# Input rows added onto folded row blocks in SBUF, gate products one per item, and four steps later in their queues

## The chip, the core and the metric

The kernel runs on one core of a Trainium2 chip. The metric is the device time of one launch in microseconds (us), the median of three runs: 2029.12 us before the change (2028.1 to 2029.63). All arithmetic is in 32-bit floats; TensorE products are made with three products of split operands (a high part and a low part), so a product in the text is often three matrix instructions.

## The reference

One layer of an encoder is computed for two sequences of 1024 rows by 1024 columns (`x_prompt`, `x_sample`):

```python
h = rmsnorm(x, g_mix) * (1.0 + sc1) + sh1
z = h @ w_in                          # q_lat 256, kv_lat 128, k_pe 64, f_in 512
y_mla = mla_group(q_lat, kv_lat, k_pe, ...)   # 4 heads, 1024 x 1024 softmax each
y_four = fourier_group(f_in, w_four)          # 2-D Fourier transform, real part
x = x + ga1 * (concatenate([y_mla, y_four]) @ w_out)
h2 = rmsnorm(x, g_ffn) * (1.0 + sc2) + sh2
ffn = (silu(h2 @ w_gate) * (h2 @ w_up)) @ w_down
out = rmsnorm(x + ga2 * ffn, g_final)
```

The shifts, scales and gates (`sh1`, `sc1`, `ga1`, ...) come from a conditioning vector of each sequence.

## The kernel before

There are five stages. Stage 1 normalises x and projects it. Stage 2 (to about 304 us) makes the Fourier part, already multiplied by its rows of `w_out` and by the gate, and stores it to DRAM as `fo_d`, 1024 x 1024 for each sequence. Stage 3 (about 304 to 720 us) is attention. Stages 4 and 5 are the feed-forward part, whose large products are made by a Strassen scheme of seven block products; it begins at about 745 us.

Stage 3 walks over 64 items: sequence s (2), block b of 256 query rows (4), head h (4), half u (2). The loop is at L1305. For item k it makes the scores (L1187 to L1221: score products in PSUM, maximum, exponential on ScalarE, reciprocal and normalisation on VectorE at L1215), turns the probabilities of an earlier item with TensorE transposes (`flip_p`, L1223), and after each pair of heads multiplies them by the values (`values`, L1237). For the heads listed in `COPIED` (L36), the probabilities first go through a copy by DMA on SyncE's queue (`pr<-p`, L1218), so that the transposes read them in another type. Meanwhile, items 3 and 4 of a block make the rotary part of the next block's queries (`rope_q`, L835, whose sum at L849 is on GpSimd), and odd items the absorbed queries (`absorb_q`, L864, tile `qa`).

The output projection of a block runs one to two blocks later (`out_step`, L1165, where i counts items from the start of the block, less one item where the block's second pair of heads is copied). It loads 128 rows of the Fourier part (`out_load`, L1118, into one of two buffers named `x2`), adds the projected attention onto it (`out_proj`, L1124, the sum at L1131 on VectorE), stores it and computes its root mean square (`norm2`, L1133: square on ScalarE, small operations of `rstd` on GpSimd), scales it (L1144; the step is kept in `S["scale"]` and taken out in the next item, L1316), and turns it for the feed-forward part (`flip_h`, L1151).

The input x has to be added to these rows. Before the change that is done in DRAM: `add_x` (L799) issues sixteen DMAs on GpSimd's queue, each adding 256 x 512 values of x onto `fo_d`. A one-element operation on the reciprocal of the item (`place`, L805) keeps each at its place in the queue, listed by item at L1300.

The gated output weights are made in stage 3 as well, once for each sequence: `gate_half` (L1251) loads half of a gate row for all partitions, `wv_load` (L1273) loads four tiles of weights and multiplies each by it on GpSimd (L1279), and `wv_split` (L1282) splits the products into high and low parts on ScalarE and VectorE. The combinations for the Strassen scheme of the first sequence are made by `comb_h` (L1255) on GpSimd, in two steps an item apart.

At the end of stage 3 the last block of the second sequence is treated apart: `x3_load` (L1405) loads its rows, `norm3` (L1424) normalises them, and `flip2` (L1442) turns the rows of the block before it, between the four output projections of the last block (loop at L1484). Its result goes through a tile `H40` that is written again soon after.

What sets the order: every engine and every DMA queue works in order. The order in a queue is made when the kernel is built, by a planner that takes what is ready first in its own estimate and goes by program order only among what is ready; so a DMA without anything to wait for can stand far ahead of its place in the program. `tc.issue_after(ins)` ties the instructions of its block behind `ins`, but only those that are on the same engine as `ins`. `here[...]` keeps the last instruction of a kind: `here["nb"]` and `here["v"]` are on VectorE, `here["exp"]` and `here["a"]` on ScalarE, `here["p"]` on GpSimd, `here["pe"]` on TensorE.

Of the kernel before, what the change touches and what calls it, by code (L numbers as in the profile page):

```python
# [12 lines left out]
F32 = mybir.dt.float32  # L13
# [3 lines left out]
ALU = mybir.AluOpType  # L17
# [4 lines left out]
P = 128  # L22
# [31 lines left out]
def hybrid_encoder_kernel(ctx: ExitStack, tc: tile.TileContext, a: dict):  # L54
# [741 lines left out]

    S = {}

    def add_x(i):  # L799

        s, b, g = i // 8, i // 2 % 4, i % 2
        bs = slice(256 * b, 256 * b + 256)
        gs = slice(512 * g, 512 * g + 512)
        pc = tiny.tile([P, 1], F32, name="pc")
        place = nc.gpsimd.tensor_tensor(out=pc, in0=S["rr"], in1=S["rr"], op=ALU.add).ins  # L805
        with tc.issue_after(place):
            nc.gpsimd.dma_start(fo_d[s][bs, gs], xs[s][bs, gs], accum_op=ALU.add)

    def half(name):
        return e.tile([P, 512], F32, tag="hv", name=name, bufs=2)  # L810
# [307 lines left out]
    def out_load(s, b, u):  # L1118
        r0 = (2 * b + u) * P
        x2 = tl.tile([P, D], F32, tag="x2", name="x2", bufs=2)  # L1120
        nc.sync.dma_start(x2, fo_d[s][r0 : r0 + P, :])
        S["x2", s, b, u] = x2
# [40 lines left out]
            nc.sync.dma_start(h2_d[s][:, 4 * g : 4 * g + 4, r0 : r0 + P], ht)  # L1163

    def out_step(s, b, i):  # L1165
        if i in (9, 11):
            out_load(s, b, i // 2 - 4)
        if i in (10, 12, 15, 16):
            n = (10, 12, 15, 16).index(i)
            out_proj(s, b, n // 2, n % 2)  # L1170
        if i in (12, 16):
            norm2(s, b, i // 4 - 3, tl, True)
        if i in (14, 19):
            flip_h(s, b, int(i == 19))

    with ExitStack() as st:
# [96 lines left out]
        def wv_load(s, g):  # L1273
            gs = slice(512 * g, 512 * g + 512)
            raw4 = (w if s == 0 else e).tile([P, 4, 512], F32, tag=f"lat{1 - s}{g}", name="wvr4")
            for h in range(HEADS):
                raw = raw4[:, h, :]
                nc.sync.dma_start(raw, wo_d[:, h, gs])
                nc.gpsimd.tensor_tensor(out=raw, in0=raw, in1=S["ga"], op=ALU.mult)  # L1279
                S["wv", h, g] = raw  # L1280

        def wv_split(i):  # L1282
            h, g = i % 4, i // 4
# [2 lines left out]
                split(wv[0][:, h, gs], wv[1][:, h, gs], S.pop(("wv", h, g)))  # L1286

        todo = {k: [] for k in range(nit)}
        for g in range(2):
            todo[2 * g].append(lambda g=g: gate_half(0, g))  # L1290
            todo[2 * g].append(lambda g=g: wv_load(0, g))
            todo[34 + 3 * g].append(lambda g=g: gate_half(1, g))
            todo[34 + 3 * g].append(lambda g=g: wv_load(1, g))
        for i in range(8):
            todo[40 + i // 2].append(lambda i=i: wv_split(i))
            todo[3 + i].append(lambda i=i: wv_split(i))
        for c, k in enumerate((49, 51, 57, 59)):
            todo[k].append(lambda c=c: comb_h(0, c))
            todo[k + 1].append(lambda: S.pop("comb")())
        for i, k in enumerate((6, 8, 10, 12, 17, 18, 19, 25, 26, 27, 33, 34, 35, 41, 42, 43)):  # L1300
            todo[k].append(lambda i=i: add_x(i))
        for u in range(2):
            todo[60 + u].append(lambda u=u: out_load(1, 2, u))

        for k in range(nit + 4):  # L1305
            if k >= nit:
                i = k - nit
                out_proj(1, 2, i // 2, i % 2)
                S["tail", i] = here["v"]
                if i == 1:  # L1310
                    norm2(1, 2, 0, tl)
                    S["tail", 5], S["tail", 6] = here["n"]
            if k < nit:
                s, b, h, u = items[k]
                scores(s, b, h, u)
                if "scale" in S:  # L1316
                    with tc.issue_after(here["nb"]):
                        S.pop("scale")()
                if k == nit - 1:
                    with tc.issue_after(here["exp"]):  # L1320
                        nc.scalar.activation(tiny.tile([P, 1], F32, tag="pc", name="warm"), cmask[:, 0:1], AF.Silu)
                nxt = items[k + 8 - k % 8] if k + 8 - k % 8 < nit else None
                i = k % 8
                if nxt is not None:
                    if i == 0:
                        load_q(*nxt[:2])
                    if i == 3 and nxt[1] == 0:
                        load_seq(nxt[0], [w.tile([P, 2, N], F32R, tag=f"lat1{i}", name=f"lat1{i}") for i in range(2)])
                    if i in (3, 4):
                        rope_q(*nxt[:2], i - 3, gbank)  # L1330
                    if i in (5, 6):
                        rope_flip(*nxt[:2], i - 5, tbank("pqt", F32R))
                if u == 1 and k + 1 < nit:
                    absorb_q(*items[k + 1][:3], gbank)
            for q in sorted({(k - 6) // 4, (k - 5) // 4}):
                if q >= 0 and k == (nit + 2 if q == nit // 4 - 1 else 4 * q + 5 + (q in COPIED)):
                    values(*divmod(q // 2, 4), q % 2)
                if k == nit + 2:
                    S["tail", 4], S["tail", 7] = here["v"], here["a"]
            for j in (k - 2, k - 1):  # L1340
                if 0 <= j < nit and j == k - 1 - (j // 4 in COPIED):
                    flip_p(*items[j])
                if k == nit:
                    S["tail"] = here["a"], here["v"]
            for n in (k // 8 - 1, k // 8 - 2):
                if 0 <= n < NOUT:
                    out_step(*divmod(n, 4), k - 8 * n - (2 * n + 1 in COPIED))
            for f in todo.get(k, ()):
                f()

    with ExitStack() as st:
# [53 lines left out]
        def x3_load():  # L1405
            X1 = quad("X1").rearrange("p a b -> p (a b)")
            for u in range(2):
                xn = X1[:, D * u : D * u + D]
                x2 = tl.tile([P, D], F32, tag="o0", name="x3", bufs=3) if u == 0 else xn
                nc.sync.dma_start(x2, fo_d[1][(6 + u) * P : (7 + u) * P, :])  # L1410
                S["x2", 1, 3, u] = x2
                S["xn", 1, 3, u] = xn

# [70 lines left out]
        for n in range(4):  # L1484
            out_proj(1, 3, n // 2, n % 2)
            if n == 1:
                norm3(0)
            if n == 2:
                fw = [tl.tile([P, 2, 512], F32R, tag=f"o{i}", name=f"fw{i}", bufs=3 - i) for i in range(2)]
                for i in range(2):  # L1490
                    split(fw[0][:, i, :], fw[1][:, i, :], w0[i])
            prep_step((2, 0, 1, 0)[n])
            if n == 1:
                hts = quad("H40")
                chained(flip2, 2, [S.pop(("xn", 1, 2, u)) for u in range(2)], lambda: tbank("pht").rearrange("p a b -> p (a b)"),
                        lambda g: hts[:, g, :])
                hts = None
# [493 lines left out]
```

## Time and profile before

| | before |
|---|---|
| median of three runs | 2029.12 us (2028.1 to 2029.63) |
| profiled execution | 2030.94 us |
| its span, first to last instruction | 2029.2 us |
| TensorE busy | 1981.6 us |
| VectorE, ScalarE, GpSimd busy | 1414.1, 896.7, 833.5 us |
| HBM read, written | 256.46 MB, 120.39 MB |
| mean granted TensorE clock | 0.994 |

In the rows, PE is TensorE, PEld its weight loads, DVE VectorE, ACT ScalarE, POOL GpSimd, SP SyncE; a q behind a name is the queue in which that engine issues DMAs. L1131 is line 1131 of the kernel. A timeline row has the start and the duration in us, the engine, the line, the operation, what it writes and reads, how many were merged, and in brackets the idle time of the engine before it with what ended that. A stretch row has the stretch, its length, the busy time and number of instructions of PE, PEld, DVE, ACT and POOL, the granted share of the TensorE clock, the share of the DMA engines' time and GB/s. A waiting row has the total, the number and the longest wait. A queue row has the number of packets, MB, and the share of the sixteen DMA engines' time. An issue row has the size and the median time from issue to landing.

### The profile page before, as it was taken

To read this page: it belongs to the slowest core of one execution; us is meant where nothing else is said; L and a number is where in the kernel's file an instruction comes from. 1 tells how busy PE (TensorE), PEld (TensorE's weight loads), DVE (VectorE), ACT (ScalarE), POOL (GpSimd) and SP (SyncE) were. 2 spreads that over 40 slices of the span, in tenths; PEclk is the share of its full clock that TensorE was granted. 3 is DMA by queue.
4 is the path that set the end of the run, shared out by engine and by line. 5 is a ranking of instruction groups with operands and counts; after the bars stand their busy time and mean duration, and the time that the engine had idled before them with its cause. 6 is when DMAs were issued, how large, how long until landed. Compare 5 with 4: busy or idle time off the path is not lost.

```text
span 2029.2 us, 28475 instructions
## 1 busy us (share of the span) xinstructions
PE 1981.6 (98%) x9840; PEld 1617.7 (80%) x9840; DVE 1414.1 (70%) x2088; ACT 896.7 (44%) x1733; POOL 833.5 (41%) x1013
## 2 busy tenths in 40 slices
PE   8899999999999999999999999999999999999997
PEld 7688877788887777888888888877788888888876
DVE  5677758676676779888677587677756655657684
ACT  4565545455465564333333364453333333336451
POOL 2454123112313327879878411233654454410142
PEclk9999999999999999999999999999999999999999
DMA  9685793667674575555555597664422322358762
GB/s 376 208 290 170 255 346 105 195 187 206 170 209 136 183 279 193 198 167 195 198 174 195 166 311 249 221 224 148 141 93 103 115 93 103 113 182 274 227 225 89
DMA packets 187725, 391.32 MB, mean 193 GB/s; under 512 B 19196, under 2 KB 58876, under 8 KB 183484
## 3 DMA queue, kind: packets, MB, share of 16 engines
q1 hardware_dynamic: 168908, 331.69, 48.4%
q0 software_dynamic: 18672, 57.81, 9.7%
q8 instruction: 77, 1.26, 0.3%
q14 instruction: 68, 0.56, 0.1%
HBM read 256.46 MB, written 120.39 MB: 186 GB/s over the span
## 4 chain that ended last, share of the span: by engine, by line
PE 55%; DVE 2%; DMA 2%; POOL 1%; issue 1%; ACT 0%; SPq 0%; DVEq 0%; ACTq 0%; POOLq 0%
PE bank L85 18%; PE bank L84 18%; PE bank L86 18%; DVE wl L64 1%; DMA draw<-t_d 1%; DVE val L144 1%; POOL val L144 1%; DMA val<-x_d 0%; DVE val L1788 0%; ACT wh L63 0%; POOL rs_y L111 0%; DMA draw<-s_d 0%; DVE val L1762 0%; SPq L1747 0%; DVE val L1777 0%
## 5 line engine op out<-in xcount | busy, mean ns | idle before, releaser
L84 PE MATMUL bank<-H,wh 128*128 128x512 f32 x1224 | 477.3, 390 | 5.3 <-DVE val L144 5.3
L86 PE MATMUL bank<-H,wl 128*128 128x512 f32 x1224 | 476.3, 389 | 0.2 <-DVE wl L64 0.2
L85 PE MATMUL bank<-H,wh 128*128 128x512 f32 x1224 | 476.3, 389 | 0.0
L144 DVE TENSOR_TENSOR val<-bank,val 128x512 f32<-128x512 f32 x244 | 166.8, 688 | 172.0 <-PE bank L86 169.1
L84 PEld LDWEIGHTS bank<-H,wh 128*128 128x128 f32 x1224 | 229.7, 188 | 56.3 <-DVE val L144 6.9
L86 PEld LDWEIGHTS bank<-H,wl 128*128 128x128 f32 x1224 | 229.8, 188 | 48.9 <-DVE wl L64 1.0
L85 PEld LDWEIGHTS bank<-H,wh 128*128 128x128 f32 x1224 | 229.8, 188 | 47.3
L64 DVE TENSOR_TENSOR wl<-draw,wh 128x512 fp32r<-128x512 f32 x286 | 202.3, 740 | 86.1 <-ACT wh L63 85.4
L63 ACT CAST wh<-draw 128x512 fp32r<-128x512 f32 x286 | 169.0, 620 | 159.9 <-PE bank L85 86.3
L85 PE MATMUL bank<-wl,wh 128*128 128x512 f32 x572 | 223.8, 391 | 3.6 <-DVE wl L64 3.6
L144 POOL TENSOR_TENSOR val<-val 128x512 f32<-128x512 f32 x58 | 84.3, 1461 | 339.9 <-DVE val L1762 189.2
L86 PE MATMUL bank<-wh,wl 128*128 128x512 f32 x572 | 222.7, 389 | 0.0
L84 PE MATMUL bank<-wh 128*128 128x512 f32 x572 | 222.6, 389 | 0.0
L63 ACT CAST wh<-rgu 128x512 fp32r<-128x512 f32 x171 | 106.3, 623 | 248.7 <-PE bank L85 192.3
L64 DVE TENSOR_TENSOR wl<-val,wh 128x512 fp32r<-128x512 f32 x133 | 134.9, 1016 | 70.8 <-ACT wh L63 70.5
L64 DVE TENSOR_TENSOR wl<-rgu,wh 128x512 fp32r<-128x512 f32 x171 | 165.3, 967 | 5.3 <-ACT wh L63 5.3
L63 ACT CAST wh<-val 128x512 fp32r<-128x512 f32 x133 | 82.3, 622 | 178.9 <-PE bank L85 158.6
L141 POOL TENSOR_TENSOR val<-rgu 128x512 f32<-128x512 f32 x80 | 114.4, 1430 | 97.1 <-DMA rgu<-in_wgu_dram 83.8
L85 PEld LDWEIGHTS bank<-wl,wh 128*128 128x128 f32 x572 | 107.4, 188 | 29.6 <-DVE wl L64 7.4
L84 PEld LDWEIGHTS bank<-wh 128*128 128x128 f32 x572 | 107.4, 188 | 22.5
L86 PEld LDWEIGHTS bank<-wh,wl 128*128 128x128 f32 x572 | 107.4, 188 | 21.8
L141 POOL TENSOR_TENSOR val<-val 128x512 f32<-128x512 f32 x89 | 119.2, 1357 | 1.3
(395 smaller groups left out, 3915.2 us busy)
## 6 DMA issues: line engine op xcount, KB each, us to landing
rgu<-in_wgu_dram SPq DMA_DIRECT2D x86, 512.0 KB
draw<-s_d SPq DMA_DIRECT2D x143, 256.0 KB
s_d<-val POOLq DMA_DIRECT2D x88, 256.0 KB, 3.6
draw<-t_d SPq DMA_DIRECT2D x88, 256.0 KB
pr<-p SPq DMA_DIRECT2D x40, 512.0 KB
s_d<-val SPq DMA_DIRECT2D x66, 256.0 KB
wada<-in_wa_dram SPq DMA_DIRECT2D x16, 1024.0 KB
draw<-in_w_down_dram SPq DMA_DIRECT2D x55, 256.0 KB
```

The costliest lines, as they stand in the source:

```text
L63: here["a"] = nc.scalar.copy(hi, src).ins
L64: here["v"] = nc.vector.tensor_tensor(out=lo, in0=src, in1=rd(hi), op=ALU.subtract).ins
L84: nc.tensor.matmul(out, lh, rh, start=first, stop=False, skip_group_check=cont)
L85: nc.tensor.matmul(out, lh, rl, start=False, stop=False, skip_group_check=cont)
L86: here["pe"] = nc.tensor.matmul(out, ll, rh, start=False, stop=last, skip_group_check=cont).ins
L141: return eng.tensor_tensor(out=out, in0=x, in1=y, op=ALU.subtract).ins
L144: return eng.tensor_tensor(out=out, in0=x, in1=y, op=ALU.add).ins
```

## The change

The sum with x moves from DRAM to SBUF: after `out_load` has loaded 128 rows of the Fourier part into `x2`, `add_x` lets a DMA on GpSimd's queue add the 128 x 1024 values of x onto that tile. There are again sixteen such DMAs of 512 KB, and the one-element operations that placed the old ones are gone. `out_load` of a block's first half moves one item earlier. The rows of the last two blocks are treated in the same way.

The products with the gate leave `wv_load` and become steps of their own (`wv_gate`), listed one per item; `wv_split` follows one item later than before for the first sequence, and the second half of the gate row is loaded later.

Three steps and a turn stand later: the scaling of `norm2` in odd items goes behind the split of the absorbed queries, the second gate row goes from item 2 to 6 (and from 37 to 38), the second Strassen combination from item 51 to 53, and `flip2` of the last block from behind its second output projection to behind its third.

```diff
-    def add_x(i):
-
-        s, b, g = i // 8, i // 2 % 4, i % 2
-        bs = slice(256 * b, 256 * b + 256)
-        gs = slice(512 * g, 512 * g + 512)
-        pc = tiny.tile([P, 1], F32, name="pc")
-        place = nc.gpsimd.tensor_tensor(out=pc, in0=S["rr"], in1=S["rr"], op=ALU.add).ins
-        with tc.issue_after(place):
-            nc.gpsimd.dma_start(fo_d[s][bs, gs], xs[s][bs, gs], accum_op=ALU.add)
+    def add_x(s, u, x2):
+        nc.gpsimd.dma_start(x2, xs[s][u * P : u * P + P, :], accum_op=ALU.add)
...
     def out_step(s, b, i):
-        if i in (9, 11):
-            out_load(s, b, i // 2 - 4)
+        if i in (8, 11):
+            out_load(s, b, i // 11)
+        if i in (9, 12):
+            add_x(s, 2 * b + i // 12, S["x2", s, b, i // 12])
...
                 nc.sync.dma_start(raw, wo_d[:, h, gs])
+                S["wv", h, g] = raw
+
+        def wv_gate(i):
+            raw = S["wv", i % 4, i // 4]
+            with tc.issue_after(here["exp"]):
                 nc.gpsimd.tensor_tensor(out=raw, in0=raw, in1=S["ga"], op=ALU.mult)
-                S["wv", h, g] = raw
...
+        for i in range(8):
+            todo[2 + i + i // 4].append(lambda i=i: wv_gate(i))
+            todo[35 + i].append(lambda i=i: wv_gate(i))
         for g in range(2):
-            todo[2 * g].append(lambda g=g: gate_half(0, g))
+            todo[6 * g].append(lambda g=g: gate_half(0, g))
             todo[2 * g].append(lambda g=g: wv_load(0, g))
-            todo[34 + 3 * g].append(lambda g=g: gate_half(1, g))
+            todo[34 + 4 * g].append(lambda g=g: gate_half(1, g))
             todo[34 + 3 * g].append(lambda g=g: wv_load(1, g))
         for i in range(8):
             todo[40 + i // 2].append(lambda i=i: wv_split(i))
-            todo[3 + i].append(lambda i=i: wv_split(i))
-        for c, k in enumerate((49, 51, 57, 59)):
+            todo[4 + i].append(lambda i=i: wv_split(i))
+        for c, k in enumerate((49, 53, 57, 59)):
             todo[k].append(lambda c=c: comb_h(0, c))
             todo[k + 1].append(lambda: S.pop("comb")())
-        for i, k in enumerate((6, 8, 10, 12, 17, 18, 19, 25, 26, 27, 33, 34, 35, 41, 42, 43)):
-            todo[k].append(lambda i=i: add_x(i))
         for u in range(2):
             todo[60 + u].append(lambda u=u: out_load(1, 2, u))
+            todo[61 + u].append(lambda u=u: add_x(1, 4 + u, S["x2", 1, 2, u]))
...
                 scores(s, b, h, u)
-                if "scale" in S:
+                later = S.pop("scale", None)
+                if later and u == 0:
                     with tc.issue_after(here["nb"]):
-                        S.pop("scale")()
+                        later()
...
                 if u == 1 and k + 1 < nit:
                     absorb_q(*items[k + 1][:3], gbank)
+                    if later:
+                        with tc.issue_after(here["v"]):
+                            later()
...
                 nc.sync.dma_start(x2, fo_d[1][(6 + u) * P : (7 + u) * P, :])
+                add_x(1, 6 + u, x2)
...
             prep_step((2, 0, 1, 0)[n])
-            if n == 1:
+            if n == 2:
                 hts = quad("H40")
                 chained(flip2, 2, [S.pop(("xn", 1, 2, u)) for u in range(2)], lambda: tbank("pht").rearrange("p a b -> p (a b)"),
                         lambda g: hts[:, g, :])
```

## The prediction

> **What bounds the kernel now.** I read the page first: span, busy time and the chain that ended last.
>
> ```profile
> span 2029.2 us, 28475 instructions
> PE 1981.6 (98%) x9840; PEld 1617.7 (80%) x9840; DVE 1414.1 (70%) x2088; ACT 896.7 (44%) x1733; POOL 833.5 (41%) x1013
> PE 55%; DVE 2%; DMA 2%; POOL 1%; issue 1%; ACT 0%; SPq 0%; DVEq 0%; ACTq 0%; POOLq 0%
> ```
>
> PE is idle for 2029.2 - 1981.6 = 47.6 us in all, and the change removes no matrix product. So it is worth what it takes out of those 47.6 us, plus what PE loses to a lowered clock after a gap. The edited code runs between about 300 us (attention begins) and 750 us (feed-forward begins). A table of that part in stretches of 10 us (columns: PE, PEld, DVE, ACT, POOL busy, granted clock, DMA share, GB/s) and PE's own timeline show where it stands still; in brackets is the idle time before a row and what ended it.
>
> ```profile
> 310.00:320.00 10.00, 7.74 (x45) 5.62 (x45) 9.42 (x17) 5.21 (x10) 7.96 (x7) 1.00 0.18 62
> 320.00:330.00 10.00, 9.56 (x49) 7.67 (x50) 9.11 (x20) 6.64 (x13) 2.15 (x2) 0.83 0.09 27
> 360.00:370.00 10.00, 9.26 (x49) 7.99 (x50) 5.71 (x13) 3.48 (x7) 1.07 (x2) 0.83 0.83 195
> 650.00:660.00 10.00, 9.64 (x47) 8.14 (x48) 4.07 (x8) 4.46 (x11) 1.41 (x2) 1.00 0.81 281
> ...
> 320.44 1.30 PE L1234 MATMUL ppt<-ident,p 128*128 128x128 f32 x8 [2.01 <-DVE nb L1211]
> 360.74 0.87 PE L1234 MATMUL ppt<-identr,pr 128*128 128x128 f32 x8 [3.25 <-DMA pr<-p]
> 382.75 0.50 PE L1197 MATMUL ps_s<-lat,qa 128*128 128x512 f32 x1 [1.42 <-DVE qa L64]
> 650.36 0.66 PE L1158 MATMUL pht<-ident,xn 128*128 128x128 f32 x4 [2.70 <-DVE pt L64]
> 738.16 0.99 PE L1447 MATMUL pht<-ident,xn 128*128 128x128 f32 x7 [1.69 <-DVE xn L1144]
> ```
>
> Five gaps: 2.01 + 3.25 + 1.42 + 2.70 + 1.69 = 11.07 us. After the first two the clock falls to 0.83 of full speed over 10 us, a loss of 0.17 x 10 = 1.7 us each. The largest wait of PE that is left within reach is on DVE's sums in the feed-forward part, where nothing is edited; dense feed-forward work gives the price of a product. PE's wait list, then a stretch of 50 us:
>
> ```profile
> PE bank L84 <- DVE val L144: 5.3, 7, 1.2
> ...
> 1450.00:1500.00 50.00, 50.00 (x222) 41.43 (x221) 28.50 (x36) 14.93 (x25) 25.63 (x20) 1.00 0.24 80
> ```
>
> That is 50 / 222 = 0.225 us for a product.
>
> **The accumulations.** Sixteen instructions add 512 KB of x each. Now they go DRAM to DRAM; after the change, DRAM onto a block that has just been loaded to SBUF. The 3.25 us gap is theirs. Timeline rows of POOL and SP, the queues' share of DMA from 353 to 357 us, the issue group, and SP's own wait:
>
> ```profile
> 351.70 0.89 POOL L807 DMA_DIRECT2D fo_d<-in_x_dram  x1
> 352.40 0.52 SPq L1218 DMA_DIRECT2D pr<-p  x1
> 359.53 0.33 SPq L1121 DMA_DIRECT2D x<-fo_d  x1
> q0 software_dynamic: 156, 0.32, 73.2%
> fo_d<-in_x_dram POOLq DMA_DIRECT2D x16, 512.0 KB, 8.6
> SPq L1121 <- DMA fo_d<-in_x_dram: 6.6, 1, 6.6
> ```
>
> At 352.40 SP issues the first copy of probabilities (pr<-p, 512 KB) that the transposes need. The accumulation issued 0.7 us before has the DMA engines alone from 353 to 357: POOL's queue is the only one in that answer. The copy's reader starts at 360.74, so issue to use was 8.3 us. An undisturbed transfer of the same size is the block load at 441.48 (SP's timeline, then stretches of 1 us):
>
> ```profile
> 441.48 0.33 SPq L1121 DMA_DIRECT2D x<-fo_d  x1
> 444.00:445.00 1.00, 1.00 (x9) 0.83 (x7) 0.00 (x0) 0.15 (x1) 0.00 (x0) 1.00 0.36 143
> 445.00:446.00 1.00, 1.00 (x9) 0.92 (x8) 0.53 (x1) 1.00 (x3) 0.00 (x0) 1.00 0.00 0
> ```
>
> Its bytes are through by 445: 3.5 us. Without the accumulation the copy is there at 352.40 + 3.5 = 355.9, before PE runs dry at 360.74 - 3.25 = 357.5. Does the accumulation leave this place? The planner puts into a queue whatever is ready first:
>
> ```profile
> 342.82 0.33 SPq L815 DMA_DIRECT2D lat<-lat_d  x1
> 478.21 0.67 DVE L1131 TENSOR_TENSOR x<-x,gb 128x512 f32<-128x512 f32 x1
> ```
>
> L815 loads latents for the second sequence; it belongs to item 27 and stands here some twenty items early. The first two block loads depended on the DRAM sums (SP's 6.6 us wait). After the change they depend on nothing recent, so they and their two accumulations should move to about 305 to 330 us, where the DMA share is 0.18 and 0.09. For later blocks the load follows the freeing of its buffer, as now. The block loaded at 441.48 is first added to by the output projection at 478.21, 36.7 us later; load 3.5 + issue 0.9 + accumulation 8.6 = 13.0 us fit. What an accumulation into SBUF takes no row shows: bounds are a plain load (3.5) and the DRAM one (8.6). I take 8.6, the nearest kind; PE sees neither. Term: 3.25 + 1.7 = **4.95 us** back.
>
> The Trainium skill, "DMA: Bandwidth & Descriptors", section "SWDGE vs HWDGE vs iDMA", says that inside a DMA engine the queues of the two kinds are served in turn. By that the copy would not have stood behind the accumulation, the gap would have another cause and stay, and 4.95 us would drop out of the sum. The 73.2% row speaks against it; it is a rival below.
>
> What comes new: an accumulation now follows every later block load by 3.5 us, and a copy may fall in there. SP issues one right behind the load of 441.48:
>
> ```profile
> 445.49 0.47 SPq L1218 DMA_DIRECT2D pr<-p  x1
> 452.17 0.54 PE L1234 MATMUL ppt<-identr,pr 128*128 128x128 f32 x4
> ```
>
> Its reader starts 6.7 us after issue. Held as long as the first copy (8.3) PE waits 1.6 us. Bounds: none, or four such in the stage, 6.4 us. I take one, **1.6 us** lost, since the sixteen accumulations of now caused one gap of such a size. The sixteen one-element products that pinned the old accumulations vanish; POOL has room, nothing on the path.
>
> **The scale of norm2 in odd items.** DVE's timeline:
>
> ```profile
> 381.61 0.75 DVE L1144 TENSOR_SCALAR xn<-x,rs_r 128x1024 f32<-128x1024 f32 x1 [1.11 <-POOL rs_r L115]
> ```
>
> DVE waits 1.11 us for POOL's root, then scales for 0.75; qa's low half (L64) stands behind both, and PE waits 1.42 for it. After the change qa goes first, the scale follows. Only the first block's steps fall in odd items (its probabilities are not copied), so it is this gap alone: **1.42 us** back. The scale's reader is a transpose an item later.
>
> **The second Strassen combination** moves from item 51 to 53: two loads on SP, four POOL operations and a store on POOL. POOL's and ACT's timelines:
>
> ```profile
> 644.53 1.29 POOL L144 TENSOR_TENSOR hcb<-hca 128x512 f32<-128x512 f32 x1 [6.21 <-DMA hc_d<-hcb]
> 645.78 1.29 POOL L141 TENSOR_TENSOR hcb<-hca 128x512 f32<-128x512 f32 x1
> 647.02 1.18 POOL L849 TENSOR_TENSOR qt<-qt 128x256 f32<-128x256 f32 x1
> 648.24 0.41 ACT L852 CAST qsk<-qt 128x256 fp32r<-128x256 f32 x1 [2.52 <-POOL qt L849]
> ```
>
> The rope sum (L849) stands behind two combination operations; ACT waits 2.52 for it with a cast behind it, and the 2.70 gap of PE at 650.36 is the end of that chain. Item 53 lies behind both rope sums of its block. Two operations are 2.5 us; ACT's wait bounds it too. I take 2.3, leaving 0.4 of the gap: **2.3 us** back.
>
> **The last fold-in of transposes** (flip2, L1447) moves behind the third output projection of the final block. PE waits 1.69 for xn:
>
> ```profile
> 737.35 0.75 DVE L1144 TENSOR_SCALAR xn<-x,rs_r 128x1024 f32<-128x1024 f32 x1 [1.55 <-POOL rs_r L115]
> 739.80 4.77 SPq L1453 DMA_DIRECT2D h_d<-H  x4
> 753.12 1.98 ACT L63 CAST H<-H 128x1024 fp32r<-128x1024 f32 x2
> ```
>
> Twelve products, 12 x 0.225 = 2.7 us, now come first and cover it: **1.69 us** back. With the transposes go eight ACT operations and four SP stores; the buffer they fill is split later (I take the cast at 753.12). The last store, issued by 739.80 + 4.77 = 744.6, moves to about 747.3 and with 3.5 us lands at 750.8, 2.3 us ahead. If that cover is gone, ACT and DVE wait what is missing.
>
> **Gates and splits.** The sixteen gate products stay. They are to be one per item, but the ordering helper ties only instructions of the named one's engine, and the named one (exp) is ACT's, the product POOL's. So they run when their rows land, as now:
>
> ```profile
> 315.78 5.64 POOL L1279 TENSOR_TENSOR wvr<-wvr,gah 128x512 f32<-128x512 f32 x4 [2.04 <-DMA gah<-ga_d]
> 318.54 1.75 DVE L1215 TENSOR_SCALAR p<-p,rr 128x1024 f32<-128x1024 f32 x1
> 329.29 0.74 DVE L1215 TENSOR_SCALAR p<-p,rr 128x1024 f32<-128x1024 f32 x1
> ```
>
> Beside four products in a row DVE's normalisation takes 1.75 instead of 0.74 us, and the 2.01 gap at 320.44 waits for it. I count 0 for this: bounds +3 us lost (two more loads and accumulations in this stretch) and 2.01 + 1.7 = 3.7 us gained if they do spread. The second gate row loads on SP four items later and the splits one item later; the last split is at item 11, its projection at 12: 0.
>
> **Sum:** 4.95 + 1.42 + 2.3 + 1.69 = 10.36 back, 1.6 lost: 8.8 us less. The profiled execution took 2030.94 us (span 2029.2 and 1.7 around it), 1.8 above the median of the runs: it goes to 2022.1, the median from 2029.12 to **2020.3 us**, 0.43% less. About 0.2% (4 us) is what a measurement here can tell from no change.
>
> The Trainium skill, "TensorE: Matmul & The Clock Gate", section "What's actually happening", lets the clock fall after an idle window of some 3.4 us. By that the 3.25 gap would cost no clock and the sum would be 1.7 smaller; the rows show 0.83 after 2.01 and 3.25 and 1.00 after 2.70, so I keep the 1.7.
>
> **Rivals.**
> - *The first gap stays*, because queues share the engines: 10.36 - 4.95 = 5.4, so 2023.7 us, on the edge of what can be told. For: sixteen accumulations, one such gap. Against: 73.2%.
> - *Given back*: four copies late (6.4) and one clock fall (1.7): 10.36 - 8.1 = 2.3, so 2026.9 us, no change.
> - *The gates do spread*: 3.7 more, 2016.6 us. Against: nothing ties them.
> - *POOL waits*, the slower side. An accumulation on POOL must wait for its load, and what stands behind it waits too. Place:
>
> ```profile
> 471.70 0.34 SPq L1121 DMA_DIRECT2D x<-fo_d  x1
> 474.93 0.73 POOL L849 TENSOR_TENSOR qt<-qt 128x256 f32<-128x256 f32 x1 [6.05 <-DVE qt L848]
> ```
>
> If the accumulation stands ahead of this rope sum, the sum comes after 471.70 + 3.5 + 0.9 = 476.1, 1.2 us late; put ahead by a whole load, 4.4 us late. PE loses what ACT waits (2.52 gave 2.70), so up to 4.6, with a clock fall 6.3 each. From two such on the gain of 8.8 is gone: 2032.9 us. Against: the planner would have to expect the load sooner than it lands.
>
> **How the numbers follow.** Forecast 0.48; first gap stays 0.13; given back 0.16; gates spread 0.12; POOL waits 0.11. Faster by over 0.2%: 0.48 + 0.12 + 0.08 (of the first rival) = 0.68; slower 0.11; between 0.21. Range 2014 to 2029: from the gates' case with no copy lost to the given-back case and small losses; it leaves out POOL's waits and little else.
>
> **What would show it.** Right: no PE wait for pr of over 1 us near 357, clock 1.00 after it; qa's split ahead of the scale; no ACT wait of 2.5 us for qt near 645; flip2 without a gap; the gate products still in rows of four. Wrong: PE waits for pr<-p in later blocks, DVE or ACT waits for POOL behind an accumulation, or the gap near 357 with no accumulation beside it.

## The result, and the profile after

The change makes the kernel slower. The changed kernel takes 2045.36 us (median of six runs, 2043.54 to 2047.36) where the kernel before took 2030.92 beside it: ratio 1.0071, 95% interval 1.0058 to 1.0084. The forecast was 2020.3 us, 0.43% less. First the head of the page of the changed kernel, its span and busy times.

```profile
span 2043.8 us, 28486 instructions
PE 1989.7 (97%) x9840; PEld 1623.6 (79%) x9840; DVE 1410.4 (69%) x2088; ACT 897.0 (44%) x1733; POOL 824.8 (40%) x997
```

PE is idle for 2043.8 - 1989.7 = 54.1 us, 6.5 more than before, and its busy time has grown by 8.1 us for the same 9840 instructions, which goes with a lower clock (mean granted share 0.988, before 0.994). Where this happens is read from marks that both kernels have. VectorE makes one score maximum for each of the 64 items, and ScalarE's first copy of the feed-forward part ends the stage. The groups by operation give the first and last start of the maxima, first of the kernel before, then of the changed one:

```profile
L1210 DVE TENSOR_REDUCE mx<-ps_s x64: 1205/1224/1226, 304.8 to 712.5; 128x1 f32<-128x1024 f32 x64
```

```profile
L1205 DVE TENSOR_REDUCE mx<-ps_s x64: 1205/1224/1226, 307.1 to 723.4; 128x1 f32<-128x1024 f32 x64
```

The differences between starts of the maxima of items 10, 13, 15, 51, 54, 63 and that copy give a table by stretch (us). The third column is the changed kernel minus the one before; "edit" names what of the change falls there.

| stretch | before | after | difference | edit |
|---|---|---|---|---|
| start to item 0 | 304.75 | 307.13 | +2.38 | none |
| item 0 to 10 | 52.78 | 52.23 | -0.55 | gates, first loads |
| 10 to 13 | 21.54 | 16.36 | -5.18 | first copy, accumulation |
| 13 to 15 | 15.50 | 19.51 | +4.01 | later scale, splits |
| 15 to 51 | 240.91 | 241.71 | +0.80 | accumulations |
| 51 to 54 | 26.36 | 25.76 | -0.60 | combination, accumulation |
| 54 to 63 | 50.66 | 60.66 | +10.00 | combination |
| 63 to first copy | 35.80 | 38.18 | +2.38 | last fold-in |
| to the end | 1280.86 | 1282.21 | +1.35 | none |

In the profiles of all kernels told of below, the first row lies between 303.1 and 307.4 and the last between 1280.2 and 1285.8 us, also where neither was edited; these two say nothing of the change. Nor does the -0.55 of item 0 to 10: kernels with nothing edited there show 50.8 to 52.9 us. The seven rows between sum to +10.86 us.

PE's timeline of the changed kernel shows the waits behind the rows, and its stretches of 10 us the granted clock (the first number behind the busy times):

```profile
378.99 0.50 PE L1190 MATMUL ps_s<-lat,qa 128*128 128x512 f32 x1 [1.67 <-ACT qa L63]
...
649.06 0.66 PE L1151 MATMUL pht<-ident,xn 128*128 128x128 f32 x4 [1.06 <-DVE pt L64]
...
680.03 0.72 PE L1229 MATMUL ppt<-identr,pr 128*128 128x128 f32 x4 [6.77 <-DMA pr<-p]
...
749.62 0.70 PE L84 MATMUL gb<-wv,o0b 128*128 128x512 f32 x1 [2.40 <-DVE x L1124]
```

```profile
360.00:370.00 10.00, 10.00 (x59) 8.21 (x58) 8.52 (x19) 6.05 (x12) 0.74 (x1) 1.00 0.15 59
380.00:390.00 10.00, 10.00 (x32) 6.98 (x31) 4.24 (x7) 1.79 (x3) 0.94 (x1) 0.66 0.73 194
670.00:680.00 10.00, 3.26 (x20) 2.16 (x19) 3.29 (x6) 3.94 (x10) 0.84 (x2) 0.90 0.86 297
680.00:690.00 10.00, 9.97 (x50) 8.44 (x50) 5.77 (x11) 4.75 (x9) 0.89 (x1) 0.76 0.70 175
750.00:760.00 10.00, 10.00 (x47) 8.18 (x47) 7.44 (x9) 5.02 (x10) 3.37 (x8) 0.84 0.57 205
```

The wait of 3.25 us for the first copy is gone and the clock there is 1.00: the row of -5.18. Two of the other gaps that the prediction took up are not gone but have another cause. For qa PE now waits 1.67 us for ScalarE where it waited 1.42 for VectorE, and the clock behind it falls to 0.66 over 10 us, 3.4 us more. The 1.69 us for xn have become 2.40 us for a PSUM bank, and 1.6 us of clock. The 2.70 us at 650 are down to 1.06, but at 680 there is a new wait of 6.77 us for a copy, and the clock falls to 0.90 and 0.76. PE stands still until 680.03, so only the second of these costs time, 2.4 us; with a wait of 0.85 us at 668.33 that is 10.0 us, beside the +10.00 of its row. The wait of 2.01 us near 320 stayed (2.09).

### The profile page after: what moved, and what is told of

Read it like the earlier page. It is cut to its first block, busy times and chain, and to the rows that moved or that the text cites. A ratio compares the mean times of both kernels' runs of the same rounds, so it can differ in the third digit from the quotient of the medians.

```text
span 2043.8 us, 28486 instructions
## 1 busy us (share of the span) xinstructions
PE 1989.7 (97%) x9840; PEld 1623.6 (79%) x9840; DVE 1410.4 (69%) x2088; ACT 897.0 (44%) x1733; POOL 824.8 (40%) x997
## 4 chain that ended last, share of the span: by engine, by line
PE 55%; DVE 2%; DMA 1%; POOL 1%; issue 1%; ACT 0%; SPq 0%; DVEq 0%; ACTq 0%; POOLq 0%
PE bank L85 19%; PE bank L84 18%; PE bank L86 18%; DVE wl L64 1%; DVE val L144 0%; DMA draw<-t_d 0%; DMA draw<-s_d 0%; ACT wh L63 0%; DVE val L1794 0%; POOL val L144 0%; POOL rs_y L111 0%; DMA rgu<-in_wgu_dram 0%; DMA val<-x_d 0%; SPq L1754 0%; DVE val L141 0%
## 5 line engine op out<-in xcount | busy, mean ns | idle before, releaser
L64 DVE TENSOR_TENSOR wl<-val,wh 128x512 fp32r<-128x512 f32 x133 | 130.2, 981 | 72.7 <-ACT wh L63 72.5
L85 PEld LDWEIGHTS bank<-wl,wh 128*128 128x128 f32 x572 | 107.3, 188 | 28.2 <-DVE wl L64 5.9
```

What stands on the lines that cost most here:

```text
L64: here["v"] = nc.vector.tensor_tensor(out=lo, in0=src, in1=rd(hi), op=ALU.subtract).ins
L85: nc.tensor.matmul(out, lh, rl, start=False, stop=False, skip_group_check=cont)
```

## The experiments

Each edit was made alone, the two large losses were taken out of the changed kernel by what was thought to cause them, and two versions keep what gained. Ratios are to the kernel before on the same chip, with 95% intervals. The stretches are those of the table above.

| kernel | median us | ratio | 10-13 | 13-15 | 15-51 | 51-54 | 54-63 | 63-copy |
|---|---|---|---|---|---|---|---|---|
| before | 2030.9 to 2033.5 | 1 | 21.54 | 15.50 | 240.91 | 26.36 | 50.66 | 35.80 |
| changed | 2045.36 | 1.0071 | 16.36 | 19.51 | 241.71 | 25.76 | 60.66 | 38.18 |
| combination alone | 2039.16 | 1.0033 (1.0020, 1.0047) | 22.56 | 15.51 | 240.78 | 23.71 | 60.72 | 35.78 |
| last fold-in alone | 2035.51 | 1.0009 (1.0000, 1.0019) | 21.96 | 15.47 | 241.01 | 27.91 | 50.68 | 38.02 |
| later scale alone | 2029.42 | 0.9987 (0.9976, 0.9998) | 22.56 | 14.39 | 240.75 | 27.79 | 50.70 | 35.78 |
| accumulation alone | 2038.45 | 1.0028 (1.0017, 1.0040) | 16.27 | 17.41 | 242.11 | 34.43 | 50.72 | 35.82 |
| gates alone | 2036.76 | 1.0012 (1.0002, 1.0021) | 21.93 | 18.59 | 240.68 | 28.14 | 50.70 | 35.79 |
| changed, combination at 51 | 2043.88 | 1.0053 (1.0035, 1.0071) | 16.36 | 17.94 | 241.73 | 34.15 | 50.71 | 36.97 |
| changed, loads tied | 2033.81 | 1.0003 (0.9993, 1.0013) | 16.36 | 17.92 | 241.67 | 23.74 | 53.54 | 38.05 |
| accumulation, tied on POOL | 2029.74 | 0.9985 (0.9973, 0.9996) | 16.26 | 15.86 | 240.59 | 27.61 | 50.69 | 35.78 |
| last fold-in, sum first | 2034.13 | 1.0005 (0.9995, 1.0014) | 21.92 | 15.52 | 240.67 | 28.20 | 50.66 | 36.43 |
| changed without gates | 2041.20 | 1.0043 (1.0026, 1.0059) | 16.29 | 14.73 | 242.26 | 25.76 | 60.81 | 38.17 |
| kept gains, item 53 | 2024.72 | 0.9959 (0.9944, 0.9973) | 16.29 | 14.73 | 240.43 | 23.74 | 51.92 | 35.79 |
| kept gains, item 52 | 2028.02 | 0.9977 (0.9964, 0.9990) | 16.29 | 14.74 | 240.43 | 23.74 | 54.05 | 35.81 |

Where nothing is edited, a stretch repeats to some 0.3 us, or differs by what the clock or a copy lost: in 51 to 54, the kernel before shows 26.36, four others with the same code there 27.8 to 28.2, since the clock fell behind their wait of 2.5 to 2.9 us.

**The combination: loads that stand ahead of a copy.** One edit to the kernel before:

```diff
-        for c, k in enumerate((49, 51, 57, 59)):
+        for c, k in enumerate((49, 53, 57, 59)):
```

> The kernel before with one edit: the second Strassen combination at item 53 in place of 51. Theory A (order on SP): in the changed kernel the loads of the next combination stand on SP ahead of a copy of probabilities, wait there for POOL to be done with the one before, and then share the DMA engines with the copy. SP's order is the same in this kernel, so PE should wait 5 to 8 us for pr near 680 us, and what follows loses 1 to 3 us of clock; the wait of 2.70 at 650.36 is gone. Net 4 to 8 us slower, ratio 1.002 to 1.004. Theory B (accumulations): the long wait of the changed kernel comes from the accumulations into SBUF that share the engines with that copy. They are not in this kernel, so no wait of over 2 us for pr near 680, and the kernel gains the 2.3 us that the prediction gave this step: ratio 0.999.

The wait is there without any accumulation into SBUF, 7.01 us, so theory A holds. Rows of POOL, SP and PE of this kernel:

```profile
667.84 1.30 POOL L141 TENSOR_TENSOR hcb<-hca,hcb 128x512 f32<-128x512 f32 x1
669.17 0.81 SPq L1259 DMA_DIRECT2D hca<-h_d  x2
669.44 0.66 POOL L1269 DMA_DIRECT2D hc_d<-hcb  x1 [0.30 <-POOL hcb L141]
670.08 0.47 SPq L1218 DMA_DIRECT2D pr<-p  x1
679.22 0.72 PE L1234 MATMUL ppt<-identr,pr 128*128 128x128 f32 x4 [7.01 <-DMA pr<-p]
```

POOL's last operation on the second combination ends at 669.14. Only then does SP issue the two loads of the third combination, which need its buffers, and the copy behind them. The copy then shares the DMA engines with 1 MB of loads ahead of it in its queue and a 1 MB store of POOL (the engines' share is 0.98 to 1.02 from 672 to 680), and its reader starts 9.1 us after issue. The step does gain what it was meant to: 51 to 54 takes 23.71 us.

To show that it is these loads in the changed kernel too, they were tied behind the latest copy:

```diff
-                nc.sync.dma_start(rd(pr), p)
+                here["pr"] = nc.sync.dma_start(rd(pr), p).ins
...
+            with tc.issue_after(here["pr"]):
                 for i in range(2):
                     nc.sync.dma_start(A[:, 2 * i : 2 * i + 2, :], h2_d[s][:, c + 4 * i, :].rearrange("p (a b) -> p a b", a=2))
```

> The changed kernel with the two loads of every Strassen combination tied on SP behind the latest copy of probabilities. Theory A: the wait of 6.77 us for pr near 680 comes from the loads of the third combination, which stand ahead of that copy on SP until POOL is done with the second and then share the DMA engines with it. With the tie the wait falls below 1.5 us and the clock there is 1.00: 7 to 9 us faster than the changed kernel, 2035 to 2039 us, ratio 1.002 to 1.0035 to the kernel before. Theory B: the copy is held up by the accumulation and the store on POOL's queue, which stay; then a wait of over 4 us stays near 680 and the time is 2042 to 2047 us.

SP and PE of that kernel:

```profile
662.24 4.82 SPq L1213 DMA_DIRECT2D pr<-p  x2
...
669.45 3.17 SPq L1255 DMA_DIRECT2D hca<-h_d  x2
...
674.47 0.85 PE L1229 MATMUL ppt<-identr,pr 128*128 128x128 f32 x8 [1.38 <-DMA pr<-p]
```

The wait falls from 6.77 to 1.38 us, the stretch from 60.66 to 53.54, and two lines of order take the changed kernel from 1.0071 to 1.0003. That is more than the 7 to 9 us that were expected; 1.6 us of it are the clock in 13 to 15, and 2.0 us lie in 51 to 54.

**The accumulation: POOL waits for a load.** The edit is the part of the change with `add_x` and `out_load`, nothing else of it.

```diff
-        if i in (9, 11):
-            out_load(s, b, i // 2 - 4)
+        if i in (8, 11):
+            out_load(s, b, i // 11)
+        if i in (9, 12):
+            add_x(s, 2 * b + i // 12, S["x2", s, b, i // 12])
```

> The kernel before with one edit: x is accumulated onto the blocks in SBUF, with their loads at items 8 and 11 of a block. Theory A (the prediction's term): the wait of 3.25 us for pr near 360 is gone and the clock is 1.00 behind it, some 5 us; later copies give back 0 to 2 us: 3 to 5 us faster, ratio 0.9975 to 0.9985. Theory B: the accumulations behind every block load hold up later copies, so that PE waits over 1 us for pr in two or more later blocks and the gain is gone: ratio 1.000 or above.

Neither theory. The first copy gains all that was predicted (21.54 to 16.27), and PE waits for no later copy. In 13 to 15 the kernel loses 1.9 us: the wait for qa is 1.67 us there, for VectorE as before, and the clock falls behind it. And 51 to 54 loses 8 us, with a wait that ends on VectorE. Rows of SP, POOL, ACT, DVE and PE:

```profile
633.07 0.81 SPq L1254 DMA_DIRECT2D hca<-h_d  x2
...
633.99 0.36 SPq L1114 DMA_DIRECT2D x<-fo_d  x1
...
644.80 0.88 POOL L800 DMA_DIRECT2D x<-in_x_dram  x1 [10.78 <-DMA x<-fo_d]
645.38 1.05 POOL L842 TENSOR_TENSOR qt<-qt 128x256 f32<-128x256 f32 x1
646.46 0.40 ACT L845 CAST qsk<-qt 128x256 fp32r<-128x256 f32 x1 [8.76 <-POOL qt L842]
646.90 2.25 DVE L846 TENSOR_TENSOR qsk<-qt,qsk 128x256 fp32r<-128x256 f32 x1 [9.00 <-ACT qsk L845]
649.07 0.74 DVE L1210 TENSOR_SCALAR p<-p,rr 128x1024 f32<-128x1024 f32 x1
649.96 1.94 PE L1229 MATMUL ppt<-ident,p 128*128 128x128 f32 x8 [7.24 <-DVE p L1210]
```

The block's load is issued at 633.99 behind 1 MB of loads for the combination, and lands only by 644.8. POOL issued a store of 1 MB at 633.35 besides, and from 634 to 642 the DMA share is 0.96 to 1.01. POOL waits 10.78 us for the load at the accumulation, with the rope sum behind. ACT waits for the sum, DVE for ACT, and behind that DVE operation stands the normalisation of the probabilities that PE wants. The test ties the accumulation behind POOL's latest rope sum or root:

```diff
-        nc.gpsimd.dma_start(x2, xs[s][u * P : u * P + P, :], accum_op=ALU.add)
+        with tc.issue_after(here["p"]):
+            nc.gpsimd.dma_start(x2, xs[s][u * P : u * P + P, :], accum_op=ALU.add)
```

> The kernel before with x accumulated onto the blocks in SBUF, each accumulation tied on POOL behind the latest rope sum or root. Without the tie that kernel had a wait of PE of 7.24 us for p at 649.96. Theory A: POOL waits 10.78 us for the block's load at the accumulation, and the rope sum behind it is what ACT, DVE and at last PE wait for. With the tie the rope sum runs first, the wait near 650 is at most the 2.70 of the kernel before, and the whole is 2 to 6 us faster than before: ratio 0.997 to 0.999. Theory B: the transfers themselves are late (the load, the loads of the combination and its store share the engines), so that a wait of over 4 us stays between 640 and 670, whatever stands first on POOL: ratio 1.001 to 1.003.

POOL's rows there:

```profile
642.62 1.18 POOL L843 TENSOR_TENSOR qt<-qt 128x256 f32<-128x256 f32 x1
643.77 1.26 POOL L141 TENSOR_TENSOR hcb<-hcb,hca 128x512 f32<-128x512 f32 x1
644.98 0.86 POOL L801 DMA_DIRECT2D x<-in_x_dram  x1
```

The accumulation does not wait at all, 51 to 54 is 27.61 as without the edit, and the kernel is faster than before, 0.9985. The tie also moved that block's load ahead of the combination's loads on SP (625.53 against 630.28), so which of the two did more was not separated.

**The two losses exclude each other.** The changed kernel with the combination back in its place:

```diff
-        for c, k in enumerate((49, 53, 57, 59)):
+        for c, k in enumerate((49, 51, 57, 59)):
```

> The changed kernel with the second Strassen combination back at item 51. Theory A (the two losses exclude each other): PE's wait of 6.77 us for pr near 680 is gone, but the accumulation of item 52 waits on POOL some 10 us for its load, the rope sum stands behind it, and PE waits about 7 us for p near 650: 2041 to 2048 us, ratio 1.0055 to 1.008 to the kernel before, no change to the changed kernel. Theory B (the losses add): the step costs its 8 us alone, and without it the kernel takes 2035 to 2038 us, ratio 1.002 to 1.0035.

Theory A, with a ratio just below the band it gave. The wait near 680 is gone (54 to 63 takes 50.71), and near 650 stands one of 6.94 us (51 to 54 takes 34.15). At item 53 the combination's loads come later, so the block's load lands earlier, and the same POOL wait is short:

```profile
642.09 0.88 POOL L800 DMA_DIRECT2D x<-in_x_dram  x1 [5.83 <-DMA x<-fo_d]
642.67 1.05 POOL L842 TENSOR_TENSOR qt<-qt 128x256 f32<-128x256 f32 x1
643.76 0.41 ACT L845 CAST qsk<-qt 128x256 fp32r<-128x256 f32 x1 [3.79 <-POOL qt L842]
```

These are rows of the changed kernel: 5.83 us on POOL, 3.79 on ACT, and on PE the 1.06 shown above and 0.41. So the five single ratios add up to +0.69%, near the +0.71% of the whole, by chance: the accumulation's 8 us are not in the whole, and the combination's gain and the scale's are not either.

**The scale and the gates.** The scale alone:

```diff
-                if "scale" in S:
+                later = S.pop("scale", None)
+                if later and u == 0:
                     with tc.issue_after(here["nb"]):
-                        S.pop("scale")()
+                        later()
...
                     absorb_q(*items[k + 1][:3], gbank)
+                    if later:
+                        with tc.issue_after(here["v"]):
+                            later()
```

> The kernel before with one edit: in odd items the scale of norm2 stands behind the split of qa on DVE. Theory A: on ACT the cast of qa still stands ahead of the exponential here, as in the kernel before, so the wait of 1.42 us at 382.75 goes and none takes its place: the items behind it come 1.4 us earlier. Theory B: the later scale itself is what turned that wait into the one of 1.67 us for ACT's cast in the changed kernel, with a clock down to 0.66 over 10 us; then a wait of over 1 us for qa shows here too, ended by ACT, and the items behind it come 0.5 to 4 us later.

Theory A: no wait for qa over 0.6 us is left, and 13 to 15 falls from 15.50 to 14.39. Then the gates alone:

```diff
+        for i in range(8):
+            todo[2 + i + i // 4].append(lambda i=i: wv_gate(i))
...
-            todo[3 + i].append(lambda i=i: wv_split(i))
+            todo[4 + i].append(lambda i=i: wv_split(i))
```

> The kernel before with one edit: the gate products one per item, the second gate row four items later, the splits one item later. Theory A: a split that comes one item later puts ACT's exponential ahead of its cast of qa near 380 us, so PE waits 1.5 to 2.5 us for qa there, ended by ACT, where before it waited 1.42 for DVE; with what the clock loses the items behind it come 0.3 to 3 us later, ratio 1.000 to 1.0015. The order on ACT is then what cost the changed kernel the gain of the later scale. Theory B (the prediction): 0, the wait at 382 stays as it was, 1.42 us and ended by DVE.

Theory A again, at its upper end: 18.59. Of the 3.1 us more, 1.7 are a lowered clock (0.85 from 380 to 390, 0.98 from 390 to 400) and 1.0 a longer standstill of PE. ACT's rows and PE's in that kernel:

```profile
383.12 1.10 ACT L1213 ACTIVATE p<-ps_s,nb 128x1024 f32<-128x1024 f32 x1
384.12 0.20 ACT L1213 ACTIVATION_READ_ACCUMULATOR p<-ps_s,nb 128x1 f32 x1
384.21 0.37 ACT L63 CAST qa<-gb 128x256 fp32r<-128x256 f32 x1
384.63 0.50 PE L1195 MATMUL ps_s<-lat,qa 128*128 128x512 f32 x1 [1.67 <-ACT qa L63]
```

In the kernel before the cast stands ahead of the exponential:

```profile
380.16 0.37 ACT L63 CAST qa<-gb 128x256 fp32r<-128x256 f32 x1 [0.20 <-PE gb L86]
380.57 1.11 ACT L1213 ACTIVATE p<-ps_s,nb 128x1024 f32<-128x1024 f32 x1
```

Only the order of the two is shown to have turned. The edit has three parts (products, row loads, splits), and which of them turned it is not separated here, nor how the planner's estimate came to it. The changed kernel without this edit:

```diff
-            todo[4 + i].append(lambda i=i: wv_split(i))
+            todo[3 + i].append(lambda i=i: wv_split(i))
```

(with the products back in `wv_load` and the gate rows at their old items.)

> The changed kernel with the gate products, their row loads and the splits as in the kernel before; all the rest of the change stays. From item 13 to item 15 the kernel before takes 15.50 us, the changed one 19.51, the one with the later scale alone 14.39, the one with the gates edit alone 18.59. Theory A (the splits, one item later, put ACT's exponential ahead of its cast of qa, and that undoes the later scale): 14.3 to 15.5 us here, no wait of PE for qa near 379, and 3 to 5 us less than the changed kernel in all: ratio 1.0045 to 1.006 to the kernel before. Theory B (the accumulations and the copies shift ACT there): 17 us or more, and no gain.

13 to 15 takes 14.73 instead of 19.51 us; in two other kernels with the later scale and the gates edit it takes 17.9, so some 1.6 us of the difference are the clock. In all it is 0.28% less than the changed kernel by the two ratios, whose intervals just touch. The gates' products themselves did not spread (their rows of four stand in the next section).

**The last fold-in.** Alone:

```diff
-            if n == 1:
+            if n == 2:
                 hts = quad("H40")
```

> The kernel before with one edit: the last fold-in of transposes (flip2) behind the third output projection of the final block. Theory A: the wait of 1.69 for xn is gone, but the first product of the last output projection waits 2 to 2.5 us for a PSUM bank, because DVE's sum stands behind DVE's scale, which waits for POOL's root, and the clock falls by some 1.6 us after it: net 1 to 2.5 us slower, ratio 1.0005 to 1.001. Theory B (the prediction): the transposes have twelve products ahead of them, no new wait comes up, and the end of attention is 1.7 us earlier: ratio 0.999. Both are at the edge of what the times tell apart; the trace between 735 and 760 us decides.

Theory A: the wait for xn is gone, one of 2.40 us for a bank has come, and the stretch takes 38.02. Then the same edit with DVE's first sum ahead of the scale:

```diff
-        norm2(1, 2, 1, xb)
+        norm2(1, 2, 1, xb, True)
...
+            if n == 0:
+                with tc.issue_after(here["v"]):
+                    S.pop("scale")()
```

> The kernel before with the last fold-in of transposes behind the third output projection, and with the scale of the last norm2 put behind the first sum of that projection on DVE. Without this second edit, PE waited 2.40 us for a PSUM bank at 739.95, and from the last score maximum to ACT's first copy of the feed-forward part it took 38.02 us, against 35.80 in the kernel before. Theory A: the bank is late because DVE's sum stands behind the scale, which waits 1.56 us for POOL's root. With the sum first the bank is there, the wait falls below 0.8 us, and the stretch takes 34.0 to 35.0 us, since the wait of 1.69 for xn is gone too. Theory B: the bank is late because DVE's splits ahead of the sum are; then the wait stays above 1.5 us and the stretch at 37 us or more.

DVE's and PE's rows, first with the fold-in alone, then with the sum first:

```profile
738.55 0.75 DVE L1144 TENSOR_SCALAR xn<-x,rs_r 128x1024 f32<-128x1024 f32 x1 [1.56 <-POOL rs_r L115]
739.22 0.68 DVE L1131 TENSOR_TENSOR x<-x,gb 128x512 f32<-128x512 f32 x1
739.95 0.80 PE L84 MATMUL gb<-wv,o0b 128*128 128x512 f32 x1 [2.40 <-DVE x L1131]
```

```profile
735.82 0.68 DVE L1131 TENSOR_TENSOR x<-x,gb 128x512 f32<-128x512 f32 x1
737.46 0.75 DVE L1144 TENSOR_SCALAR xn<-x,rs_r 128x1024 f32<-128x1024 f32 x1 [0.96 <-POOL rs_r L115]
738.12 2.35 DVE L64 TENSOR_TENSOR H<-H,H 128x1024 fp32r<-128x1024 f32 x2
740.39 0.68 DVE L1131 TENSOR_TENSOR x<-x,gb 128x512 f32<-128x512 f32 x1
741.13 0.50 PE L84 MATMUL gb<-wv,o0b 128*128 128x512 f32 x1 [0.69 <-DVE x L1131]
```

The wait of 2.40 us is the scale's: it goes. But the stretch is 36.43 and not below 35: the next bank waits 0.69 us behind two splits of 2.35 us, and the transposes 0.72 for ACT to read theirs. Both theories had a part, and the step gains nothing over the 35.80 of the kernel before.

**What is worth keeping.** Accumulation tied on POOL, later scale, combination's loads tied behind the copy; gates, splits and last fold-in as before. With the combination at item 53, then at 52:

> A version meant to be faster than both: the kernel before with the accumulation into SBUF (each one on POOL behind the latest rope sum or root), the later scale, the second Strassen combination at item 53, and the loads of the combinations behind the latest copy of probabilities on SP; gates, splits and the last fold-in as before. From the stretches of the other runs (item 10 to 13: 16.3 against 21.5; 13 to 15: 14.4 against 15.5; 51 to 63: 77.3 against 77.0): 5 to 7 us faster than before, ratio 0.9965 to 0.998. If the parts disturb each other, PE waits over 2 us for p or pr near 650 or 675, and the ratio is 0.999 or more.

> The same with the second Strassen combination at item 52 in place of 53, so that its first two operations stand on POOL between the rope sums and the next root, where POOL has nothing to do for 13 us. If the combination costs PE nothing there, the 2.70 wait of the kernel before near 650 goes and the waits of 0.86 and 1.38 us of item 53 near 663 and 674 do not come: 1 to 3 us faster than with item 53, ratio 0.995 to 0.997. If the loads, which come only behind the copy, are late for it, POOL waits for them with the root behind it, and it is 0 to 3 us slower than with item 53.

At item 53 the ratio is 0.9959, faster than both kernels, by 0.41% of the kernel before, a little more than expected. With item 52 the gain that was expected did not come: 54 to 63 is 2.1 us longer and the ratio 0.9977. POOL waits for the loads until 651.58 there, as the worse of the two cases had it, but 1.7 of the 2.1 us are the clock, which fell to 0.83 between 660 and 670 behind two waits of 0.65 and 0.83 us.

## Why the prediction was wrong, step by step

- **First copy, 4.95 us back: right.** 5.18 here, and all eight kernels with the edit take 16.3 us where those without it take 21.5 to 22.6. So the rival that the gap stays is out. It was drawn from the Trainium skill, "DMA: Bandwidth & Descriptors", section "SWDGE vs HWDGE vs iDMA" (a DMA engine serves the two kinds of queues in turn); these rows do not bear out that reading of it.
- **One late copy by accumulations, 1.6 us: wrong place.** With the tie on POOL PE waits for no later copy over 0.6 us. The +0.80 of items 15 to 51 goes with the tie as well (240.59). Taken was 8.6 us for an accumulation into SBUF; its issue row in the changed kernel (last number: median from issue to landing, where it is known) says 5.9:

```profile
x<-in_x_dram POOLq DMA_DIRECT2D x15, 512.0 KB, 5.9
```

- **The rival "POOL waits": real, with too small a price.** It was given one chance in nine and 4.4 us of lateness at most, from an undisturbed load of 3.5 us. The load took 10.8 us from issue to POOL's start, because the combination's loads stood ahead of it in the queue and a 1 MB store ran beside it, and PE lost 7.24. The argument against it, that the planner would have to expect the load sooner than it lands, was no argument: it did. In the whole change it is nearly covered, through the later combination.
- **Scale, 1.42 us back: right alone (1.11), wrong in the whole.** The failing step is the next one.
- **Gates and splits, 0: wrong, 3.1 us alone (15.50 to 18.59).** That nothing ties the products was right; POOL still does them four in a row. But the splits were costed by when their result is needed (item 12), not by what the edit does to the order on ACT: it changed which of two ACT instructions comes first. That it was the splits, and not the row loads or the products, is argued and not shown. The bound of 3 us lost that the prediction gave was for loads and accumulations, so that it met the size is luck.

```profile
309.56 5.98 POOL L1279 TENSOR_TENSOR wvr<-wvr,gah 128x512 f32<-128x512 f32 x4 [3.62 <-DMA wvr<-wo_d]
...
318.93 5.60 POOL L1279 TENSOR_TENSOR wvr<-wvr,gah 128x512 f32<-128x512 f32 x4 [2.71 <-DMA gah<-ga_d]
```

- **Combination, 2.3 us back: the gain right (2.65 from 26.36 to 23.71, and 4.1 to 4.5 against the kernels whose clock fell behind that wait), the cost missed, 10 us.** The prediction named the two loads on SP that move with the step. It did not ask which loads wait for the buffers that the step now frees later, those of the third combination, nor what stands behind them on SP. This is the largest failing step. It did not decide the sign alone: with those loads tied the changed kernel is at 1.0003, so the other losses (gates, fold-in) had about used up the gains, and with the combination back at item 51 the wait of POOL takes its place.
- **Last fold-in, 1.69 us back: wrong, 2.2 lost.** Twelve products were to cover the transposes, but a product needs a free bank, and DVE's sum that frees it stood behind the very scale that the transposes waited for. The wait was moved to another reader of the same late root.
- **Signs.** Those named as right that came true: no wait near 357 and the clock 1.00 behind it, qa's split ahead of the scale (at 379.58 and 380.02), products in rows of four, the fold-in's own gap gone. Those that failed: ACT waits 3.79 us for qt, behind an accumulation, and a later pr<-p holds PE; both were named as signs of error.

## What to carry to other kernels

When a step moves later in a queue that works in order, follow its buffers too: here the next user's loads waited for them at the head of a DMA queue and held a copy behind them, 7 us of PE. A DMA that had to wait for another transfer held up the engine that issues it (POOL, 10.78 us), so it belongs behind the small operations that other engines want, and its wait is to be sized by the bytes ahead of that transfer and beside it, not by an undisturbed load. An edit that gains alone can be undone by another, and losses can hide each other, so a sum of single results is checked by stretches.

## What the runs showed of the hardware

A gap of the same size at the same place cost clock in one run and none in another: behind 1.67 us at 378.99 the changed kernel's clock was 0.66 over 10 us (3.4 us lost), behind 1.68 us at the same place with the tied accumulation it was 1.00, as the row says; behind waits of 2.0 to 2.3 us near 320 it was 0.83 in some kernels and 1.00 in others.

```profile
380.00:390.00 10.00, 10.00 (x55) 7.84 (x54) 5.16 (x9) 3.36 (x6) 0.00 (x0) 1.00 0.56 190
```

Finer stretches show more. The first two rows are the kernel before around its wait of 2.01 us near 320, the last three around its wait of 2.70 us near 650:

```profile
317.71:321.12 3.41, 1.40 (x11) 0.99 (x10) 3.41 (x8) 0.73 (x1) 3.41 (x3) 1.00 0.00 0
321.13:324.53 3.40, 3.40 (x12) 2.36 (x12) 3.15 (x7) 2.25 (x6) 1.02 (x2) 0.50 0.24 77
...
645.39:648.79 3.40, 2.27 (x15) 1.75 (x13) 1.96 (x3) 0.88 (x4) 3.40 (x4) 1.00 0.00 0
648.80:652.21 3.41, 1.85 (x13) 1.68 (x14) 3.03 (x5) 3.14 (x10) 2.54 (x3) 1.00 0.17 24
652.22:655.62 3.40, 3.40 (x17) 2.82 (x16) 0.92 (x2) 1.91 (x4) 0.00 (x0) 1.00 0.88 326
```

In all fourteen profiles the clock from 300 to 780 us is either 1.00 or 0.50; the 0.83 and 0.66 of stretches of 10 us are averages of the two. It is 0.50 for one, two or three times 3.41 us, up to 1.7 us lost each, and within a run these stretches begin whole multiples of 3.41 us apart. Each run was cut into steps of 3.41 us on that grid. Each of the 30 steps at full clock in which PE stood still for 1.8 us or more is followed by a lowered step; of the 36 with 1.2 to 1.8 us, 6 are; with less, none is. So 2.01 us inside one step cost 1.7 us, and the 2.70 us, cut by the border at 648.80 into 1.13 and 1.56, cost nothing. Why steps with 1.2 to 1.8 us, such as those with the two gaps near 379 above, go both ways stays open.

The Trainium skill, "TensorE: Matmul & The Clock Gate", section "What's actually happening", has a free-running window of some 3.4 us that halves the clock when it was idle. The trace agrees on the window, on its running free and on the half. But 1.8 to 2.8 us of standstill were enough in most of these falls, and a gap of 1.67 us cannot fill a window either, so a window idle throughout is not the condition that these rows show.
